# A hybrid decoder step on one core: the first head's q and k of the second attention half loaded in the decode stage

## The chip, the cores and the metric

One Trainium2 chip, one of its cores. The time is device microseconds of one launch of the whole step. Three timed runs of the kernel before gave 1573.43, 1573.64 and 1575.61 us; their median is 1573.64 us.

## The reference

One layer of a decoder. Each token vector (1024 prompt tokens and 8 x 4 sample tokens, 1024 wide) is normalised, modulated and multiplied by one combined input weight, which gives q, k and v of eight attention heads and the inputs of a gated linear recurrence (HGRN). The attention of one head:

```
z = (q @ k.T) * scale + bias_head          # q and k were normalised per head
log_1m = where(key < query, log_sigmoid(-z), 0)
tail   = sum of log_1m over the later keys of the row
w      = where(key < query, exp(log_sigmoid(z) + tail), 0)
o      = w @ v
```

The sample tokens attend to 1024 cached keys each, which lie in pages of 128 keys in DRAM (the decode). Then an output projection with residual, a second norm, and a squared-ReLU MLP (1024 to 4096 to 1024) with residual.

## The kernel before

Every matrix product runs in float32 split into a high and a low part, as three matmuls. The prompt is worked on in two halves of 512 tokens. After q, k and v of all tokens are computed they are put into DRAM scratch: `qkd[part, hi/lo, pair, 128, T]` for q and k, `vd` for v. The order of the stages after that: HGRN with the attention of tokens 0 to 511; output projection of those tokens; then, interleaved, the **first MLP** (tokens 0 to 511, `mlp`, L1178) with `decode_and_attention` (L1434), which is the decode, the HGRN of the sample tokens and the attention of tokens 512 to 1023; then the second output projection and the last MLP.

The interleaving is written by hand: `interleave((mlp(...), WM), (decode_and_attention(), W[3]))` near the end of `hymba_step` draws from two generators in the proportion 64 to 166. From the program so written a planner fixes the order of each engine's instructions and each queue's DMAs beforehand, by simulated times; at run time every engine works through its own list in order. Tiles come from pools; a tile with a `tag` and `bufs=2` has two buffers that later tiles of the tag take in turn when all readers are done. Pools that follow one another lie in the same memory, so a load into a new pool's tile waits for the readers of whatever old tile lay there.

What the change touches:

- `attention` (L874): for each of 8 heads it loads `qh` and `ql` (high and low part of q, 256 KB each, the 64 rows of the head written to both halves of the partitions), `kk` (both parts of k, 512 KB) and `vhl` (v, 512 KB), all issued on GpSimd's queue (L886, L887, L889). Each of the four tiles has two buffers in the pool `attn1`. Then for each block of 128 queries the products `pz` (L900, L901), two sigmoids on ScalarE (L904, L905), masks on GpSimd (L908, L909), a running product on VectorE (L914) and its use on GpSimd (L915), the transposes `ptw` (L927) and the products with v (L936, L937).
- `attn1` lies over the decode's pool: the second buffer of `ql` lies over `ms`, the decode's result, which leaves by the DMA of L696.
- `decode` (L561): GpSimd clears `qbd` (L564), VectorE fills it (L568); pages of 256 KB come on SyncE's queue into four buffers `raw` (L614), are transposed on TensorE (L630) and multiplied with `qbd` (L636).
- `hgrn_decode` (L957): for each of four pairs of heads a transpose `pks` (L991), its copy `kts` by ScalarE (L993) and the products `pds` (L1001) that need it.
- The pool `res` (L1460) beside the first MLP: `xres`, two buffers of 2 KB per partition for the residual in the MLP's last block (L1234, L1235), and `g2b`, 4 KB per partition, the gate (L1183, loaded at L1213). Before they are loaded for that use they lie empty. One buffer of `xres` and part of `g2b` lie over the output projection's last tiles (`hf`, read by L334).
- `weight` (L154): weights come on SyncE's queue (L161) and are split by ScalarE (`whi`, L151) and VectorE or GpSimd (`wlo`, L152).

Of the kernel before, what the change touches and what calls it, by code (L numbers as in the profile page):

```python
# [9 lines left out]
F32 = mybir.dt.float32  # L10
F32R = mybir.dt.float32r
# [9 lines left out]
P = 128  # L21
D = 1024
KT = 8
T = 1024
# [9 lines left out]
NBE0, NBE, NHB, NWA, NU, NRW, NX2, NF = 4,8,3,4,4,4,3,3  # L34
# [47 lines left out]
def hymba_step(ctx, tc, x_p, x_s, ck, cv, st_in, ptab, c_p, c_s, w_ada, b_ada, n1g, n2g, w_in,  # L82
# [3 lines left out]
    V, S, G, TE = nc.vector, nc.scalar, nc.gpsimd, nc.tensor  # L86
# [14 lines left out]
    def pool(name, side="left", stack=ctx, **kw):  # L101
        return stack.enter_context(tc.tile_pool(name=name, bufs=1, side=side, reuse_waits="tile", **kw))
# [7 lines left out]
    qkd = dp.tile([2, 2, 4, P, T], F32, name="qkd")  # L110
# [39 lines left out]
    def split(hi, lo, src, e=None, h=None):  # L150
        (V.tensor_copy if h is V else S.copy)(hi, src)  # L151
        (e or V).tensor_tensor(lo, src, hi.bitcast(F32), op=sub)  # L152
# [34 lines left out]
    def side_by_side(*steps):  # L187

        steps = [[g, n, 0] for g, n in steps]
        while steps:  # L190
            x = min(steps, key=lambda x: (x[2] + 0.5) / x[1])
            if next(x[0], x) is x:
                steps.remove(x)
            else:
                yield
            x[2] += 1
# [38 lines left out]
    def bank(kind, shape, name):  # L235
        turn[kind] = turn.get(kind, -1) + 1
        tag = banks[kind][turn[kind] % len(banks[kind])]
        return psum.tile(shape, F32, name=name, tag=f"bank{tag}", bufs=1)
# [632 lines left out]
        with tc.high_priority(offset=PH):  # L871
            norm()

    def attention(pb, ms, nbe):  # L874

        q0, nq, nk = 256 * ms[0], 256 * len(ms), 256 * (ms[-1] + 1)
        both = lambda t, part, p, r, cs: qkd[t, part, p, r, cs].unsqueeze(0).to_broadcast([2, 64, cs.stop - cs.start])
        for p in range(4):
            for hh in range(2):
                h = 2 * p + hh  # L880
                hr = slice(64 * hh, 64 * hh + 64)

                qh, ql = (pb.tile([P, nq], F32R, name=name, bufs=2) for name in ("qh", "ql"))
                kk_ = pb.tile([P, nk], F32R, name="kk", bufs=2)
                for part, tile_ in enumerate((qh, ql)):
                    G.dma_start(tile_, both(0, part, p, hr, slice(q0, q0 + nq)))  # L886
                G.dma_start(kk_, qkd[1, :, p, hr, 0:nk])  # L887
                vhl = pb.tile([P, nk // P, P], F32R, name="vhl", bufs=2)
                G.dma_start(vhl, vd[0:nk, P * h:P * (h + 1)].rearrange("(t p) x -> p t x", p=P))  # L889
                for m in ms:  # L890
                    ws = []
                    for i in (2 * m, 2 * m + 1):
                        n = (i + 1) * P
                        row, right = [], None
                        for c in reversed(range(0, n, 512)):
                            e = min(n, c + 512)
                            w = e - c
                            pz = bank("z", [P, 512], "pz")[:, :w]
                            qs_ = slice(i * P - q0, (i + 1) * P - q0)
                            TE.matmul(pz, qh[:, qs_], kk_[:, c:e], start=True, stop=False)  # L900
                            TE.matmul(pz, ql[:, qs_], kk_[:, c:e], start=False, stop=True)  # L901
                            om = pb.tile([P, 513], F32, name="om", bufs=NOM)
                            be = pb.tile([P, 512], F32, name="be", bufs=nbe)
                            S.activation(om[:, 0:w], pz, AF.Sigmoid, bias=sbn[:, h:h + 1], scale=-1.0)  # L904
                            S.activation(be[:, 0:w], pz, AF.Sigmoid, bias=sbp[:, h:h + 1])  # L905
                            if right is None:
                                causal = dict(pattern=[[-1, P]], compare_op=ALU.is_gt, base=0, channel_multiplier=1)
                                G.affine_select(om[:, w - P:w], om[:, w - P:w], fill=1.0, **causal)  # L908
                                G.affine_select(be[:, w - P:w], be[:, w - P:w], fill=0.0, **causal)  # L909
                                G.memset(om[:, w:w + 1], 1.0)  # L910
                            else:
                                G.tensor_copy(om[:, w:w + 1], right[:, 0:1])
                            back = om[:, 0:w][:, ::-1]
                            V.tensor_tensor_scan(back, back, back, 1.0 if right is None else right[:, 0:1], op0=mult, op1=ALU.bypass)  # L914
                            G.tensor_tensor(be[:, 0:w], be[:, 0:w], om[:, 1:w + 1], op=mult)  # L915
                            row.insert(0, be)
                            right = om
                        ws.append(row)
                    pv = bank("a", [P, 256], "pv")
                    for kb in range(0, 2 * m + 2, 2):  # L920
                        diag = kb == 2 * m
                        pt = bank("t", [P, 2, 256], "ptw")
                        for a in range(2):
                            for u in range(2):
                                if diag and a == 1 and u == 0:
                                    continue
                                TE.transpose(pt[:, a, u * P:(u + 1) * P], ws[u][kb // 4][:, (kb % 4 + a) * P:(kb % 4 + a + 1) * P], ident)  # L927
                        wh = pb.tile([P, 2, 256], F32R, name="wh", bufs=NWH)
                        wl = pb.tile([P, 2, 256], F32R, name="wl", bufs=NWH)
                        parts = [(slice(0, 1), slice(0, 256)), (slice(1, 2), slice(P, 256))] if diag else [(slice(0, 2), slice(0, 256))]  # L930
                        for a, cs in parts:
                            split(wh[:, a, cs], wl[:, a, cs], pt[:, a, cs], h=V if (kb // 2) % SPL == SPL - 1 else S)
                        for a in range(2):
                            cs = slice(P, 256) if diag and a == 1 else slice(0, 256)
                            vs = vhl[:, kb + a, :]
                            TE.matmul(pv[:, cs], vs, wh[:, a, cs], start=(kb == 0 and a == 0), stop=False)  # L936
                            TE.matmul(pv[:, cs], vs, wl[:, a, cs], start=False, stop=(diag and a == 1))  # L937
                    tv = pb.tile([64, 256], F32, name="tv", bufs=1)
                    S.copy(tv, pv[64:128])
                    V.tensor_tensor(tv, pv[0:64], tv, op=add)  # L940
                    nc.sync.dma_start(mixa[m][64 * h:64 * h + 64, :], tv)
                    yield
# [14 lines left out]
    def hgrn_decode(p1):  # L957
# [63 lines left out]
        for j in range(4):  # L1021
# [10 lines left out]
             lambda n, p=ga: p.tile([P, 2048], F32, name="wada", bufs=NAR)[:, 0:512 * n], "ada")  # L1032
# [4 lines left out]
    qstack.close()  # L1037
    gh = hgrn(pool("hgrn", stack=gstack))
    gb = attention(pool("attn0", stack=astack), (0, 1), NBE0)

    def until(g, x):
# [136 lines left out]
    def mlp(h_hi, h_lo, chunks, fp, nx, side=iter(())):  # L1178
# [1 line left out]
        r_hi = [h_hi[:, k] for k in range(KT)]  # L1180
        r_lo = [h_lo[:, k] for k in range(KT)]
        n = chunks[-1].stop
        g2b = fp.tile([P, D], F32, name="g2b")  # L1183
        acc = [lp.tile([P, HW], F32, name=f"acc{c}", tag="acc", bufs=8) for c in range(KT)]
        for blk in range(NBLK):
            u_hi, u_lo, ws = [], [], []
# [20 lines left out]
            if blk == 0:  # L1207
                for cs in parts:
                    for m in range(NK):
                        up(m, cs)  # L1210
                    yield
            if blk == NBLK - 1:
                nc.sync.dma_start(g2b, g2d.to_broadcast([P, D]))  # L1213
            for half_ in range(2):

# [217 lines left out]

    def decode_and_attention():  # L1434
        banks.update(BD)
        with ExitStack() as es:
            gd = decode(pool("decode", stack=es))
            for _ in range(33):
                next(gd)
                yield  # L1440
            banks.update(BV)
            yield from side_by_side((gd, 28), (hgrn_decode(pool("hgrn_s", stack=es)), W[4]))
        banks.update(BA)
        with ExitStack() as es:
            yield from attention(pool("attn1", stack=es), (2, 3), NBE)

    def h2_tiles():
        return hp2.tile([P, KT, HW], F32R, name="h2_hi", tag="h2_hi", bufs=1), hp2.tile([P, KT, HW], F32R, name="h2_lo", tag="h2_lo", bufs=1)
# [11 lines left out]
    rp = pool("res", side="right", stack=rstack)  # L1460
    banks.update(BM)
    banks.update(m0=M0)
    gate = lambda: rp.tile([P, 512], F32, name="ar", tag="xres", bufs=2)
    ga = ada(AP1, gate, lambda n: wp.tile([P, 512 * n], F32, name="wada", tag="wraw", bufs=NWR), "m")
    interleave((mlp(*h2, [slice(0, 512)], rp, 2, ga), WM), (decode_and_attention(), W[3]))
    h2 = h2_tiles()
    banks.update(o="45", r="36", s=BS)
# [38 lines left out]
```

## Time and profile before

| | |
|---|---|
| median of three runs | 1573.64 us (1573.43 to 1575.61) |
| the profiled execution's own time | 1574.93 us |
| its span (first to last instruction) | 1573.2 us |
| TensorE busy | 1509.9 us, 96% of the span |
| VectorE, ScalarE, GpSimd busy | 1069.0, 641.9, 439.1 us |
| mean granted TensorE clock | 0.985 |
| mean DMA rate over the span | 142 GB/s |

Stages by the span's time: the first MLP with decode and attention runs from about 555 us to 1106 us; the decode's first pages are transposed at 573 us, the first product of the second attention half starts at 832 us. A row of the timeline gives the start, the length, the engine, the line, the operation, the tiles as out<-in, the shapes and, in brackets, how long the engine was idle before and what ended that. DMA issues on a queue carry SPq or POOLq. Where several equal instructions follow one another they share a row with their count.

### The profile page before, as it was taken

How to read it: one execution, taken by the hardware profiler on the slowest of the kernel's cores; microseconds unless marked ns; L12 is line 12 of the kernel's file. 1: busy time of each engine (PE TensorE's matmuls, PEld its weight loads, DVE VectorE, ACT ScalarE, POOL GpSimd, SP SyncE). 2: the span in 40 equal slices, each digit the busy share in tenths (PEclk: the TensorE clock that was granted, in tenths of full speed). 3: DMA queues.
4: the chain of work that ended last, by engine and by line, in shares of the span. 5: the costliest groups of instructions: out<-in, count | busy, mean ns of one | idle time of the engine just before them, and what ended most of it. 6: DMA issues, size and time to landing. Idle time of an engine off the chain costs nothing.

```text
span 1573.2 us, 26210 instructions
## 1 busy us (share of the span) xinstructions
PE 1509.9 (96%) x9485; PEld 1260.8 (80%) x9485; DVE 1069.0 (68%) x2216; ACT 641.9 (41%) x1219; POOL 439.1 (28%) x624
## 2 busy tenths in 40 slices
PE   6999999999999989999998999999798999999998
PEld 3666689998998877765566788888477999999998
DVE  4976438888866872444554987888487657777775
ACT  2742233444423453433232665655344533333340
POOL 0200125644210120000111776793105313331310
PEclk8999999999999999999998999999899999999999
DMA  8379873523124456667566384642743322323222
GB/s 315 121 270 308 264 221 66 111 63 78 39 73 143 135 192 217 206 221 243 157 148 124 97 144 101 133 125 83 228 136 101 104 93 82 103 73 105 84 82 85
DMA packets 249414, 223.14 MB, mean 142 GB/s; under 512 B 60507, under 2 KB 196259, under 8 KB 247236
## 3 DMA queue, kind: packets, MB, share of 16 engines
q1 hardware_dynamic: 186308, 199.26, 40.2%
q0 software_dynamic: 62976, 22.20, 8.2%
q8 instruction: 75, 1.23, 0.3%
q14 instruction: 55, 0.45, 0.1%
HBM read 190.14 MB, written 31.11 MB: 141 GB/s over the span
## 4 chain that ended last, share of the span: by engine, by line
PE 67%; DVE 12%; issue 10%; DMA 6%; ACT 2%; POOL 2%; SPq 0%; POOLq 0%; ACTq 0%; DVEq 0%
PE pm L204 10%; PE pm L205 10%; PE pm L206 10%; PE pm_qkv L217 3%; PE pm_qkv L215 3%; PE pm_qkv L216 3%; PE pm L1223 2%; DVE wlo L152 2%; PE pm L1224 2%; PE pm L1225 2%; PE pm_u L1307 2%; PE pm_u L1308 2%; PE pm_u L1309 2%; PE ptd L630 2%; PE ptw L927 1%
## 5 line engine op out<-in xcount | busy, mean ns | idle before, releaser
L204 PE MATMUL pm<-h_hi,whi 128*128 128x384 f32 (+3 forms) x800 | 273.6, 344 | 7.4 <-DVE h_hi L333 3.3
L205 PE MATMUL pm<-h_lo,whi 128*128 128x384 f32 (+3 forms) x800 | 271.4, 340 | 0.1
L206 PE MATMUL pm<-h_hi,wlo 128*128 128x384 f32 (+3 forms) x800 | 271.2, 340 | 0.0
L151 ACT CAST whi<-wraw 128x1024 fp32r<-128x1024 f32 x136 | 142.7, 1052 | 231.5 <-PE pm L205 114.9
L152 DVE TENSOR_TENSOR wlo<-wraw,whi 128x1024 fp32r<-128x1024 f32 x128 | 171.5, 1340 | 85.4 <-ACT whi L151 76.2
L204 PEld LDWEIGHTS pm<-h_hi,whi 128*128 128x128 f32 x800 | 151.9, 191 | 29.5 <-issue 9.8
L206 PEld LDWEIGHTS pm<-h_hi,wlo 128*128 128x128 f32 x800 | 151.9, 190 | 10.4 <-issue 1.2
L205 PEld LDWEIGHTS pm<-h_lo,whi 128*128 128x128 f32 x800 | 152.0, 190 | 9.1 <-DVE h_lo L334 0.4
L205 PE MATMUL pm<-ul,whi 128*128 128x272 f32 x512 | 146.4, 289 | 2.5 <-DVE ul L1323 2.4
L204 PE MATMUL pm<-uh,whi 128*128 128x272 f32 x512 | 142.0, 290 | 5.3 <-ACT uh L1322 4.3
L206 PE MATMUL pm<-uh,wlo 128*128 128x272 f32 x512 | 145.5, 288 | 0.0
L914 DVE TENSOR_TENSOR_SCAN om<-om 128x128 f32<-128x128 f32 (+3 forms) x96 | 110.0, 1150 | 27.2 <-POOL om L908 19.0
L915 POOL TENSOR_TENSOR be<-be,om 128x384 f32<-128x384 f32 (+3 forms) x96 | 101.2, 1063 | 52.4 <-DVE om L914 43.3
L1223 PE MATMUL pm<-whi,uh 128*128 128x512 f32 x256 | 106.0, 414 | 2.4 <-DVE acc L1231 2.1
L1225 PE MATMUL pm<-whi,ul 128*128 128x512 f32 x256 | 103.0, 406 | 1.6 <-DVE ul L1196 1.6
L1224 PE MATMUL pm<-wlo,uh 128*128 128x512 f32 x256 | 102.4, 401 | 0.0
L205 PEld LDWEIGHTS pm<-ul,whi 128*128 128x128 f32 x512 | 96.3, 188 | 4.0 <-DVE ul L1323 3.9
L204 PEld LDWEIGHTS pm<-uh,whi 128*128 128x128 f32 x512 | 94.0, 188 | 6.7 <-ACT uh L1322 5.0
L206 PEld LDWEIGHTS pm<-uh,wlo 128*128 128x128 f32 x512 | 96.2, 188 | 0.1
L217 PE MATMUL pm_qkv<-whi,h_lo 128*128 128x512 f32 x192 | 77.6, 405 | 0.8 <-DVE h_lo L334 0.8
L215 PE MATMUL pm_qkv<-whi,h_hi 128*128 128x512 f32 x192 | 76.5, 401 | 1.4 <-DVE rs_i L138 1.3
L216 PE MATMUL pm_qkv<-wlo,h_hi 128*128 128x512 f32 x192 | 76.7, 399 | 0.0
(403 smaller groups left out, 3510.2 us busy)
## 6 DMA issues: line engine op xcount, KB each, us to landing
wraw<-in_w_down_dram SPq DMA_DIRECT2D x64, 512.0 KB, 4.0
wraw<-in_w_up_dram SPq DMA_DIRECT2D x40, 512.0 KB, 4.4
wada<-in_w_ada_dram SPq DMA_DIRECT2D x16, 1024.0 KB, 8.1
raw<-in_cache_k_dram SPq DMA_DIRECT2D x64, 256.0 KB, 3.3
vt<-in_cache_v_dram SPq DMA_DIRECT2D x64, 256.0 KB, 3.9
wraw<-in_w_in_dram SPq DMA_DIRECT2D x24, 512.0 KB, 5.0
uraw<-in_w_up_dram SPq DMA_DIRECT2D x24, 512.0 KB, 3.9
wa<-in_w_ada_dram SPq DMA_DIRECT2D x16, 512.0 KB, 6.5
```

What stands on the lines that cost most here:

```text
L151: (V.tensor_copy if h is V else S.copy)(hi, src)
L152: (e or V).tensor_tensor(lo, src, hi.bitcast(F32), op=sub)
L204: TE.matmul(pm, w_hi[:, k, :], r_hi[k][:, cs], start=(k == ks[0]), stop=False)
L205: TE.matmul(pm, w_hi[:, k, :], r_lo[k][:, cs], start=False, stop=False)
L206: TE.matmul(pm, w_lo[:, k, :], r_hi[k][:, cs], start=False, stop=(k == ks[-1]))
L215: TE.matmul(pm, h_hi[:, k, cs], hi, start=(k == 0), stop=False)
L216: TE.matmul(pm, h_hi[:, k, cs], lo, start=False, stop=False)
L217: TE.matmul(pm, h_lo[:, k, cs], hi, start=False, stop=(k == KT - 1))
L914: V.tensor_tensor_scan(back, back, back, 1.0 if right is None else right[:, 0:1], op0=mult, op1=ALU.bypass)
L1223: TE.matmul(pm, u_hi[m][:, ts], hi, start=(m == 0), stop=False)
L1224: TE.matmul(pm, u_hi[m][:, ts], lo, start=False, stop=False)
L1225: TE.matmul(pm, u_lo[m][:, ts], hi, start=False, stop=(m == NK - 1))
```

## The change

The three loads of the first head of the second attention half are issued at the head of `decode_and_attention`, before the decode is set up, into the two `xres` buffers (q) and the `g2b` buffer (k) of the pool `res`. `attention` takes these tiles for its head 0 and loads the other seven heads as before. The loads themselves move into a helper, `load_qk`, with the same access patterns and the same queue. `g2b` is now a tile that is made in the MLP's last block, in the place that `kk0` had. v of head 0 is loaded where it was.

```diff
@@ -871,20 +871,27 @@
-    def attention(pb, ms, nbe):
+    def load_qk(qh, ql, kk, h, q0, nq, nk):
+
+        hr = slice(64 * (h % 2), 64 * (h % 2) + 64)
+        for part, x in enumerate((qh, ql)):
+            G.dma_start(x, qkd[0, part, h // 2, hr, q0:q0 + nq].unsqueeze(0).to_broadcast([2, 64, nq]))
+        G.dma_start(kk, qkd[1, :, h // 2, hr, 0:nk])
+
+    def attention(pb, ms, nbe, first=None):
 
         q0, nq, nk = 256 * ms[0], 256 * len(ms), 256 * (ms[-1] + 1)
-        both = lambda t, part, p, r, cs: qkd[t, part, p, r, cs].unsqueeze(0).to_broadcast([2, 64, cs.stop - cs.start])
...
-                qh, ql = (pb.tile([P, nq], F32R, name=name, bufs=2) for name in ("qh", "ql"))
-                kk_ = pb.tile([P, nk], F32R, name="kk", bufs=2)
-                for part, tile_ in enumerate((qh, ql)):
-                    G.dma_start(tile_, both(0, part, p, hr, slice(q0, q0 + nq)))
-                G.dma_start(kk_, qkd[1, :, p, hr, 0:nk])
+                if h == 0 and first:
+                    qh, ql, kk_ = first
+                else:
+                    qh, ql = (pb.tile([P, nq], F32R, name=name, bufs=2) for name in ("qh", "ql"))
+                    kk_ = pb.tile([P, nk], F32R, name="kk", bufs=2)
+                    load_qk(qh, ql, kk_, h, q0, nq, nk)
...
-        g2b = fp.tile([P, D], F32, name="g2b")
...
             if blk == NBLK - 1:
+                g2b = fp.tile([P, D], F32, name="g2b", tag="g2b")
                 nc.sync.dma_start(g2b, g2d.to_broadcast([P, D]))
...
     def decode_and_attention():
         banks.update(BD)
+        first = [rp.tile([P, n], F32R, name=name, tag=tag, bufs=b)
+                 for name, n, tag, b in (("qh0", 512, "xres", 2), ("ql0", 512, "xres", 2), ("kk0", T, "g2b", 1))]
+        load_qk(*first, 0, 512, 512, T)
...
-            yield from attention(pool("attn1", stack=es), (2, 3), NBE)
+            yield from attention(pool("attn1", stack=es), (2, 3), NBE, first)
```

## Rows read from the trace of the kernel before

**Rows 1.** Waits of PE over the span: total us, times, longest.

```profile
PE pm_os L1103 <- DMA woraw<-in_w_out_dram: 8.2, 1, 8.2
PE pz L900 <- DMA kk<-qkd: 4.9, 1, 4.9
```

**Rows 2.** Timeline of PE around the start of the second attention half.

```profile
832.22 0.45 PE L900 MATMUL pz<-kk,qh 128*128 128x128 f32 x1 [4.88 <-DMA kk<-qkd]
...
833.34 1.12 PE L1001 MATMUL pds<-ve,kts 32*64 32x256 f32 x4
```

**Rows 3.** Windows there: length; busy (count) of PE, PEld, DVE, ACT, POOL; clock; DMA; GB/s.

```profile
827.34:832.22 4.88, 0.01 (x1) 0.04 (x1) 0.00 (x0) 0.92 (x1) 0.00 (x0) 0.71 0.21 57
832.22:839.65 7.43, 7.43 (x21) 5.31 (x21) 3.84 (x6) 0.91 (x4) 3.57 (x7) 0.50 0.79 166
839.65:846.23 6.58, 6.58 (x31) 4.82 (x30) 2.82 (x5) 0.98 (x1) 0.00 (x0) 1.00 1.16 140
```

**Rows 4.** Timeline of POOL: the loads of heads 0 and 1.

```profile
813.69 0.83 POOL L887 DMA_DIRECT2D kk<-qkd  x1
...
833.62 0.78 POOL L886 DMA_DIRECT2D ql<-qkd  x1 [17.32 <-DVE wlo L152]
```

**Rows 5.** DMA issues from 813.6 to 814.2: size, us from issue to landing.

```profile
kk<-qkd POOLq DMA_DIRECT2D x1, 512.0 KB, 18.4
```

**Rows 6.** Timeline of ACT: the cast and the copy ahead of L1001.

```profile
831.30 1.04 ACT L151 CAST whi<-wraw 128x1024 fp32r<-128x1024 f32 x1 [7.20 <-DMA wraw<-in_w_up_dram]
832.26 0.25 ACT L993 COPY kts<-pks 32x128 f32<-32x128 f32 x1
```

**Rows 7.** Timeline of SP: a weight of the MLP issued at 813.78.

```profile
813.78 1.02 SPq L161 DMA_DIRECT2D wraw<-in_w_up_dram  x1
```

**Rows 8.** Windows of the decode's start (columns as in Rows 3).

```profile
570.00:575.00 5.00, 5.00 (x45) 5.00 (x45) 4.78 (x21) 4.24 (x12) 3.96 (x9) 1.00 0.28 61
575.00:580.00 5.00, 5.00 (x43) 4.58 (x46) 4.83 (x11) 1.95 (x5) 0.00 (x0) 1.00 0.93 301
```

**Rows 9.** Waits of DVE from 560 to 600.

```profile
DVE qbd L568 <- POOL qbd L564: 2.1, 1, 2.1
```

**Rows 10.** Timelines of POOL and PE: the decode's setup and its first use.

```profile
566.55 1.65 POOL L334 TENSOR_TENSOR h_lo<-hf,h_hi 128x512 fp32r<-128x512 f32 x1 [8.92 <-DVE h_hi L333]
568.14 1.00 POOL L564 MEMSET qbd<- 128x1088 f32 x1
...
579.74 1.07 PE L636 MATMUL pzd<-kt,qbd 128*32 128x512 f32 x8
```

**Rows 11.** Timeline of SP: loads into the pool `res`.

```profile
568.23 0.33 SPq L1235 DMA_DIRECT2D xres<-x1d  x1
...
582.44 0.43 SPq L1213 DMA_DIRECT2D g2b<-g2d  x1
```

**Rows 12.** DMA issues near 581.1 and near 587.6: one page each.

```profile
raw<-in_cache_k_dram SPq DMA_DIRECT2D x1, 256.0 KB, 3.0
...
raw<-in_cache_k_dram SPq DMA_DIRECT2D x1, 256.0 KB, 6.4
```

**Rows 13.** Timeline of PE: pages 7 and 8, 9 and 13 transposed.

```profile
583.13 1.04 PE L630 MATMUL ptd<-ident,raw 128*128 128x128 f32 x8
...
586.79 0.60 PE L630 MATMUL ptd<-ident,raw 128*128 128x128 f32 x4
...
595.30 0.60 PE L630 MATMUL ptd<-ident,raw 128*128 128x128 f32 x4
```

**Rows 14.** DMA queues from 828 to 831: packets, MB, share of 16 engines.

```profile
q0 software_dynamic: 50, 0.14, 12.8%
q1 hardware_dynamic: 32, 0.01, 2.6%
```

**Rows 15.** The page's median for w_down, and the issue from 834.0 to 834.3.

```profile
wraw<-in_w_down_dram SPq DMA_DIRECT2D x64, 512.0 KB, 4.0
...
wraw<-in_w_down_dram SPq DMA_DIRECT2D x1, 512.0 KB, 8.9
```

## The prediction, before the changed kernel was run

> **What bounds the kernel now.** I read the page first: TensorE is busy for 96% of the span, so a change pays where TensorE stands still or runs slowly, and hardly anywhere else. The list of TensorE's waits comes next [rows 1]. Two waits are long: 8.2 us for the second output projection's weight, which the change does not name, and 4.9 us for `kk`, the k of head 0 of the second attention half. In PE's timeline that wait stands ahead of the first `pz` at 832.22 [rows 2]. The windows add what follows it [rows 3]: in the 4.88 us of the wait TensorE does next to nothing, then it is busy for all of 7.43 us at a granted clock of 0.50, which is the 1.2 GHz level, and from 839.65 on the clock is 1.00, the 2.4 GHz level. 7.43 us at half clock is 3.7 us of work at the full one. So the place costs 4.9 + 3.7 = **8.6 us**, and the change can win no more than that here.
>
> GpSimd issues this k load at 813.69 [rows 4], when the decode's memory comes free, and it lands 18.4 us later [rows 5], at 832.1. A weight of the same 512 KB has a median of 4.0 us [rows 15]. The load is slow and late at once.
>
> **What the change removes at 832.** *The wait for k:* q and k of head 0 are issued about 245 us earlier, so `pz` can start where PE comes to it, at 827.34: **-4.9**.
>
> *The half clock:* the granted clock fell behind a stretch of 4.88 us in which PE did nothing [rows 3]. Without that stretch I expect no fall: **-3.7**. Its bounds are 0 and -3.7.
>
> *What is late next:* `pds`, 1.12 us behind `pz` on PE [rows 2], needs `kts`, a copy on ScalarE. On ScalarE that copy stands behind a cast of the MLP's weight, which began at 831.30 after a wait of 7.20 us for the weight w_up [rows 6]. The weight was issued at 813.78 [rows 7] and so took 17.5 us: it went beside the q and k loads. If PE comes to `pds` at 827.34 + 1.12 = 828.46, the weight must be there by about 827.1 (less 1.04 for the cast, 0.25 for the copy). If it lands at 831.2 as before, `pds` waits until 832.5, 4.1 us, PE stands still nearly as long as before, the clock falls again, and 8.6 shrinks to 4.9 - 4.1 = 0.8. What the weight will take is not in the trace. GpSimd will issue v of head 0 and then q and k of head 1, so loads of the same kind still go beside it, each a little later. The bounds are the 17.5 us of the trace and the 8.9 us that a 512 KB weight took right behind the q and k loads of head 1 [rows 15]. I take 14.3, nearer to the upper end because the neighbours are of the same kind: it lands at 828.1 and `pds` waits **+1.0** (bounds 0 and, with the clock, 7.8).
>
> *Head 1:* its `ql` was issued only at 833.62, after GpSimd had stood for 17.32 us behind a buffer [rows 4]. The buffers turn by one place, so that wait goes to a later head, behind loads that nothing needs soon; I cost it at nothing. The cover is the output of the sample tokens' HGRN, which separates head 0's first product from the rest of the attention. Without it a late `kk` would cost a wait of up to 4.9 again.
>
> **What it adds at 568.** Three issues on GpSimd, 0.83 us each [rows 4], 2.5 us, stand ahead of the clearing of `qbd`. They cannot go before GpSimd's last `h_lo` ends, at 568.2, because one of the q buffers lies over its operand: the load of `xres` into that place was issued at 568.23, just then [rows 10, 11]. VectorE already waits 2.1 us for the cleared `qbd` [rows 9], and is busy for 4.78 of 5 and 4.83 of 5 us in the two windows [rows 8]. TensorE uses `qbd` first at 579.74 [rows 10]. The 2.5 us are mostly covered by that distance; if VectorE's list has no slack they arrive whole. I take **+0.5** (bounds 0 and 2.5).
>
> *The transfers:* 1 MB of q and k is added, where the DMA share is 0.28 until 575 and then 0.93 [rows 8]. The loads of `xres` and `g2b`, issued at 568.23 and 582.44 [rows 11], go away from there and come after head 0 has been used; the MLP's last block, which needs them, stands far behind that, and it is this distance that covers them: I cost them at nothing. Should it be short, the last block would wait one load, 4.0 us [rows 15]. Their going relieves the queue of SyncE by three issues. The pages have little room: one issued at 581.1 took 3.0 us and one at 587.6 took 6.4 [rows 12]; they were used at 586.79 and 595.30 [rows 13], which leaves 2.7 and 1.3 us. A weight beside such loads took 8.9 us for a median of 4.0 [rows 15], so they can make a transfer **4.9 us** late. Less the slack of 2.7 that is **+2.2**. The lower bound is 0: PE waits for none of these pages now, so there is nothing to win. The upper bound is the second rival's 8.9.
>
> **The sum:** -4.9 - 3.7 + 1.0 + 0.5 + 2.2 = -4.9 us. The profiled execution took 1574.93 us and would take 1570.0. The median of the runs, 1573.64, lies 1.3 below it, so I predict 1573.64 - 4.9 = **1568.7 us**. About 0.2% (3.1 us) is what a measurement of this kernel can tell from no change. By itself this case ranges from 1564.5 (all of the gain and a little from the new plan) to 1572.6 (GpSimd's 2.5 and 4.0 of late pages beside the 1.0).
>
> **Rival 1: another wait takes the place.** `pds` waits for `kts`, and this for the weight, as late as before. For it: ScalarE had already stood 7.20 us for that weight [rows 6], which landed 0.9 us before k did. Against it: the weight would no longer go beside the k of head 0. The gain is 0.8; with +0.5 and +2.2 in front the time is 1573.64 - 0.8 + 2.7 = **1575.5**.
>
> **Rival 2: slower, by the pages.** The k load takes its 18 us whatever else happens, and a page that shares its DMA engines ends only when it ends. GpSimd is free at 568.2, issues two q loads, and k at 569.9; with 18.4 us [rows 5] it lands at 588.3. Pages 7 and 8 are transposed at 583.13 [rows 13]; if they come with it, PE waits 5.2 us. The clock would fall as behind the wait of 4.88 (3.7 more), and VectorE's 2.5 would not be covered. That is 11.4, or 8.9 without the 2.5, against a gain of 8.6 - 1.0 = 7.6: +3.8, **1577.4**. It decides from a page lateness of about 4 us in excess of its slack. For it: the weight that took 17.5 us beside k [rows 6, 7] was the same size as two pages. Against it: while the k load was in the way the two queues moved 50 and 32 packets in 3 us [rows 14], so SyncE's queue kept its turn, and the DMA share at 570 to 575 is only 0.28 [rows 8].
>
> The Trainium skill speaks for this rival: the page "DMA: Bandwidth & Descriptors", in "Rules for kernel authors", says that an outermost dimension of a size c below 16 "confines the whole DMA to at most c engines". Both the q loads (two copies) and the k load (two parts) lead with a dimension of 2, so by that rule two engines would carry them, every page with a piece on either would wait there, and the time would be the 1577.4 just worked out. The trace agrees as far as it goes, 18.4 us against 4.0 for the same size [rows 5, 15]; which engines carried the load is in no row here.
>
> **Rival 3: the change does not do what it says.** The order of each engine and queue is planned afresh from simulated times behind 568. The planner may put the three loads late in the decode, or shift other work so that the gain goes into the 8.2 us wait for the output projection's weight [rows 1]. That gives 1573.6, within 3 us on either side. Against it: TensorE is nearly without a wait between the two, so what is won at 832 should arrive.
>
> **How the numbers follow.** The forecast has 0.46, rival 1 0.18, rival 2 0.22, rival 3 0.14. Faster by over 0.2%, under 1570.5: 0.37 of the forecast's 0.46 lies there, 0.02 of rival 1, 0.01 of rival 2, 0.04 of rival 3, together 0.44. Within 0.2%: 0.09 + 0.10 + 0.05 + 0.05 = 0.29. Slower: 0 + 0.06 + 0.16 + 0.05 = 0.27. The range is 1564.0 to 1578.5: it holds the forecast's own range and both rivals' times with about 1 us beyond rival 2, and leaves out pages that are later still (rival 2 with its waits twice) and large gains from the new plan.
>
> **What the profile after would show.** Right: no wait of PE for `kk` near 827, `pz` at a granted clock of 1.00, head 0's q and k issued on GpSimd at 568 to 571, landing long before use. The 1.0 is right if `pds` waits about 1 us and ScalarE's wait for w_up falls to some 4 us. The 2.2 is right if a `raw` page appears among PE's waits between 575 and 600 with about 2 us. Wrong by rival 1: a wait at `pds` of about 4 us released by `kts`, and a clock of 0.50 behind it. Wrong by rival 2: waits for `raw` of 5 us, and 0.50 in a window near 585. Wrong by rival 3: the loads issued far from 568, or a `woraw` wait longer than 8.2 by what was won.

## The result and the profile after

The changed kernel takes 1588.67 us (median of four runs) where the kernel before takes 1574.31: a ratio of 1.0086, with a 95% interval of 1.0070 to 1.0102. That is 14.4 us **slower**, where 4.9 us faster was forecast; it also lies beyond the upper end of the range, 1578.5. The profiled execution has a span of 1588.0 us, 14.8 more than before. One execution of front_spread_wh, below, took 5096.77 us and is left out of its numbers.

PE's waits over the span are the first thing to read (total us, times, longest). PE is TensorE, DVE VectorE, ACT ScalarE, POOL GpSimd and SP SyncE:

```profile
PE pm_os L1110 <- DMA woraw<-in_w_out_dram: 8.2, 1, 8.2
PE ptd L630 <- DMA raw<-in_cache_k_dram: 6.6, 3, 3.1
PE pm L1230 <- DVE acc L1238: 5.6, 3, 4.7
```

The 4.9 us for `kk` [rows 1] are gone, and with them the half clock of [rows 3]. In their place stand 6.6 us for pages of the decode, for which PE did not wait before, and 4.7 us at one time for `acc` (2.1 in all before). The wait for `woraw` is what it was.

**The front.** The DMA issues from 568 to 575 give each load's size and the us from issue to landing:

```profile
kk<-qkd POOLq DMA_DIRECT2D x1, 512.0 KB, 21.4
qh<-qkd POOLq DMA_DIRECT2D x1, 256.0 KB, 7.5
ql<-qkd POOLq DMA_DIRECT2D x1, 256.0 KB, 10.0
...
s0b<-in_state_hgrn_dram POOLq DMA_DIRECT2D x1, 64.0 KB, 18.1
```

GpSimd's issues and PE's transposes of pages, from the timelines:

```profile
569.16 0.90 POOL L878 DMA_DIRECT2D qh<-qkd  x1
...
570.86 0.79 POOL L879 DMA_DIRECT2D kk<-qkd  x1
```

```profile
583.30 0.63 PE L630 MATMUL ptd<-ident,raw 128*128 128x128 f32 x4 [3.08 <-DMA raw<-in_cache_k_dram]
...
586.79 1.09 PE L630 MATMUL ptd<-ident,raw 128*128 128x128 f32 x4 [2.50 <-DMA raw<-in_cache_k_dram]
```

The load of k is issued at 570.86, as forecast, and lands at 592.3. A load of 64 KB of the recurrence's state, issued meanwhile, takes 18.1 us. The windows (length; busy and count of PE, PEld, DVE, ACT, POOL; granted clock; DMA share; GB/s) show what PE pays; the four lines are of the changed kernel, and the line below them is the kernel before, where PE is busy without a gap from 575 to 605 at a clock of 1.00:

```profile
580.00:585.00 5.00, 1.21 (x9) 0.82 (x8) 2.83 (x12) 1.37 (x3) 0.00 (x0) 0.97 1.10 233
585.00:590.00 5.00, 3.21 (x17) 2.94 (x21) 0.69 (x1) 0.00 (x0) 0.00 (x0) 0.50 0.71 154
590.00:595.00 5.00, 5.00 (x28) 2.89 (x21) 1.05 (x1) 2.11 (x4) 0.00 (x0) 0.84 0.42 133
600.00:605.00 5.00, 3.98 (x28) 2.56 (x20) 0.84 (x2) 1.09 (x2) 0.00 (x0) 1.00 0.96 306
```

```profile
585.00:590.00 5.00, 5.00 (x29) 3.16 (x27) 1.79 (x3) 1.80 (x4) 0.00 (x0) 1.00 0.98 316
```

PE stands for 3.79 + 1.79 + 1.02 = 6.6 us. The granted clock is 0.50 for 3.21 us of work (1.6 lost) and 0.84 for 5.00 (0.8 lost). Together that is **9.0 us**. A point that both programs pass is `pzn`, products that stand in both halves of the decode. This view gives count, duration in ns, and the start of the first and the last; first the kernel before, then the changed one:

```profile
L651 PE MATMUL pzn<-kTn,qbf x16: 196/206/217, 667.2 to 744.9; 128*32 128x32 f32 x16
```

```profile
L651 PE MATMUL pzn<-kTn,qbf x16: 196/206/217, 677.0 to 759.9; 128*32 128x32 f32 x16
```

The first comes 9.8 us later, which answers to the 9.0 and to 1.0 that was there before the loads: GpSimd's last `h_lo` begins at 567.57, for 566.55 [rows 10]. The last comes 15.0 later: another **5.2 us** are lost between, where PE has no wait. Of these, 3.3 show in the products of the decode with v: PE is busy with them for 28.3 us before and 31.6 after (L680, from 600 to 830):

```profile
L680 PE MATMUL pod<-vt,wt 128*32 128x512 f32 x128 | 28.3, 602 | 0.0
```

```profile
L680 PE MATMUL pod<-vt,wt 128*32 128x512 f32 x128 | 31.6, 603 | 0.0
```

One such product takes as long as before (602 and 603 ns). 128 of them make 77 us, so they overlap in both kernels, and after the change they overlap less. They also stand in another order, which the planner set anew: on PE, runs of only two such products come 13 times, for 5 times in the kernel before. That pages come late is not the reason, as front_k_spread shows below. The other 1.9 us I cannot assign.

**The start of the second attention half.** GpSimd's timeline:

```profile
829.61 0.84 POOL L879 DMA_DIRECT2D kk<-qkd  x1
847.56 0.93 POOL L896 DMA_DIRECT2D vhl<-vd  x1 [17.11 <-DMA mixs<-ms]
...
850.05 0.34 POOL L915 TENSOR_SCALAR_AFFINE_SELECT om<-om 128x128 f32<-128x128 f32 x1
```

And VectorE's and PE's, a little later:

```profile
850.42 0.42 DVE L921 TENSOR_TENSOR_SCAN om<-om 128x128 f32<-128x128 f32 x1 [6.64 <-POOL om L915]
850.77 0.66 DVE L1238 TENSOR_TENSOR acc<-acc,pm 128x512 f32<-128x512 f32 x1
```

```profile
851.48 0.80 PE L1230 MATMUL pm<-whi,uh 128*128 128x512 f32 x1 [4.70 <-DVE acc L1238]
```

This is a chain over four engines, and is read backwards. PE waits for a bank of PSUM that VectorE's `acc` clears; `acc` stands on VectorE behind head 0's running product; that waits for head 0's mask on GpSimd; and the mask stands behind head 1's v load, which waits 17.1 us until the decode's result `ms`, over whose memory its buffer lies, has left. PE loses 4.7 us, then 1.35 more at half clock:

```profile
851.50:854.20 2.70, 2.70 (x6) 2.13 (x7) 2.05 (x4) 0.00 (x0) 0.54 (x2) 0.50 1.44 332
```

So the account of the profile is 9.0 + 5.2 in front, 8.6 won at 832 and 6.1 lost just behind it: 11.7 of the 14.8 us. Of the other 3, 1.0 was there before the loads, and 1.9 is one wait of PE at 872 for `rr`, which the kernel before does not have.

### The profile page after: what moved, and what is told of

It is laid out like the page before. It is cut to its first block, busy times and chain, and to the rows that moved or that the text cites. A ratio compares the mean times of both kernels' runs of the same rounds, so it can differ in the third digit from the quotient of the medians.

```text
span 1588.0 us, 26219 instructions
## 1 busy us (share of the span) xinstructions
PE 1516.1 (95%) x9485; PEld 1261.6 (79%) x9485; DVE 1077.5 (68%) x2216; ACT 642.9 (40%) x1219; POOL 437.1 (28%) x624
## 4 chain that ended last, share of the span: by engine, by line
PE 71%; DVE 13%; DMA 7%; issue 4%; ACT 2%; POOL 1%; SPq 0%; POOLq 0%; DVEq 0%; ACTq 0%
PE pm L204 10%; PE pm L205 10%; PE pm L206 10%; PE pm_qkv L217 3%; PE pm_qkv L215 3%; PE pm_qkv L216 3%; PE pm L1230 2%; PE pm L1232 2%; PE pm L1231 2%; PE pod L680 2%; DVE wlo L152 2%; PE pm_u L1314 2%; PE pm_u L1315 2%; PE pm_u L1316 2%; DVE om L921 2%
## 5 line engine op out<-in xcount | busy, mean ns | idle before, releaser
L206 PEld LDWEIGHTS pm<-h_hi,wlo 128*128 128x128 f32 x800 | 151.9, 190 | 12.6 <-issue 3.7
```

Source lines behind the costliest of these rows:

```text
L206: TE.matmul(pm, w_lo[:, k, :], r_hi[k][:, cs], start=False, stop=(k == ks[-1]))
```

## The experiments

Two theories were stated. **A:** the load of q and k, in the form in which it is written (a source that leads with a dimension of 2), moves on few DMA engines; whatever needs these engines meanwhile is late. **B:** head 0's masks stand on GpSimd behind a load whose buffer lies over `ms`. The rivals stand with each run. All times are set against runs of the kernel before on the same chip.

**Another form of the early loads (front_spread).** Each early load is cut in two, so that each half goes to 64 partitions and its source leads with a dimension of 64.

```diff
-    def load_qk(qh, ql, kk, h, q0, nq, nk):
+    def load_qk(qh, ql, kk, h, q0, nq, nk, spread=False):
...
+        for half in range(2):
+            for part, x in enumerate((qh, ql)):
+                G.dma_start(x[64 * half:64 * half + 64], qkd[0, part, h // 2, hr, q0:q0 + nq])
+            G.dma_start(kk[64 * half:64 * half + 64], qkd[1, half, h // 2, hr, 0:nk])
...
-        load_qk(*first, 0, 512, 512, T)
+        load_qk(*first, 0, 512, 512, T, spread=True)
```

> The changed kernel, with the three early loads of head 0 cut into six: each writes 64 partitions from a source whose leading dimension is 64. Theory A (the early k load moves on few DMA engines and holds up the cache pages): k lands within about 8 us of its issue instead of 21.4, the pages land in about 5 us, PE's 6.6 us of waits for raw and the half clock near 585 to 595 are gone, and the time falls by some 10 us to about 1578. Rival (the megabyte or the issues on GpSimd are at fault, in whatever form): the pages stay late, GpSimd has three issues more, and the time stays at 1586 to 1591.

Measured: 1572.82 us, ratio 0.9985 (0.9974 to 0.9997). The issues near 567 to 571:

```profile
kk<-qkd POOLq DMA_DIRECT2D x2, 256.0 KB, 4.1
qh<-qkd POOLq DMA_DIRECT2D x2, 128.0 KB, 3.3
ql<-qkd POOLq DMA_DIRECT2D x2, 128.0 KB, 3.4
```

The same bytes, from the same place, at the same time, by the same queue land in 3 to 4 us a piece in place of 7.5 to 21.4, with three issues more on GpSimd. PE has no wait for `raw`, and is busy throughout 575 to 605 at a clock of 1.00. The last `pzn` starts at 744.5, so the 5.2 us behind the front are gone too (L680 takes 28.3 us again), and that is why the gain was 16 us and not the 10 expected. Theory A holds. What keeps this kernel from the forecast is again `acc`: one wait of 4.1 us, behind a wait of GpSimd for `mixs` of 16.3 us.

How few the engines are, the kernel before shows already. From 828 to 831 hardly anything but k's load was left on GpSimd's queue, and the queue's packets took 12.8% of 16 engines' time [rows 14], which is the time of 2.05 engines. From 570 to 573 in front_spread they took 124.1%, the time of 20. The k load is 128 packets of 4 KB in the trace: at most three of them are under way at a time in the kernel before, mostly two, and up to 25 in front_spread. Which engines these are is in no view.

No run separates the leading dimension from the cutting itself. But a load that is not cut speaks for the dimension: in the first attention half of the kernel before, k (leading with 2) and v (leading with 128) have the same size, and each is one load on GpSimd's queue.

```profile
kk<-qkd POOLq DMA_DIRECT2D x8, 256.0 KB, 11.4
vhl<-vd POOLq DMA_DIRECT2D x8, 256.0 KB, 4.3
```

**The early loads alone (before_dead).** The kernel before, with the three early loads added, used by nobody; `g2b` moves into the MLP's last block as in the changed kernel, which the cut below leaves out.

```diff
         banks.update(BD)
+        early = [rp.tile([P, n], F32R, name=name, tag=tag, bufs=b)
+                 for name, n, tag, b in (("qh0", 512, "xres", 2), ("ql0", 512, "xres", 2), ("kk0", T, "g2b", 1))]
+        for part, x in enumerate(early[:2]):
+            G.dma_start(x, qkd[0, part, 0, 0:64, 512:1024].unsqueeze(0).to_broadcast([2, 64, 512]))
+        G.dma_start(early[2], qkd[1, :, 0, 0:64, 0:T])
```

> The kernel before, with the three early loads added at the head of the decode into the same tiles of the pool beside the MLP, but used by nobody; attention loads head 0 as it did. This prices the front alone. Theory A: waits for raw of some 6 us and half clock near 585, the wait for kk of about 5 us at 832 still there: 1573.6 + 10 = about 1584. Rival (the front costs little, and the loss of the changed kernel comes from the end of the decode and from the new plan): 1573 to 1577.

Measured: 1592.36 us, ratio 1.0104 (1.0085 to 1.0124). PE's waits over the span:

```profile
PE ptd L630 <- DMA raw<-in_cache_k_dram: 8.6, 2, 8.2
...
PE pz L900 <- DMA kk<-qkd: 3.1, 1, 3.1
```

The front alone costs 16 us by the ratio, 18 by the medians, in this plan, more than expected: one wait of 8.2 us, half clock behind it, and an order of the decode in which L680 takes 33.0 us. The rival, that the front costs little, is out.

**q or k (front_k_spread).** Of the early loads only k's is cut in two.

> The changed kernel, with only the early k load cut into two of 64 partitions each; the two early q loads keep their form. It tells whether k or q held up the pages. Theory A by size (k is 512 KB on few engines, each q load half of that and on few engines as well): the q loads still take 7 to 11 us and make the first pages late, the waits for raw fall from 6.6 to 0 to 3 us: 1574 to 1580. If k alone was at fault: 1572 to 1574, as with all six. If q alone: 1584 to 1589.

Measured: 1582.54 us, ratio 1.0044 (1.0025 to 1.0063); PE still waits 5.0 us for `raw` (in the trace of 1578.47 us, the fastest of the seven runs). The issues from 565 to 573:

```profile
kk<-qkd POOLq DMA_DIRECT2D x2, 256.0 KB, 13.9
...
qh<-qkd POOLq DMA_DIRECT2D x1, 256.0 KB, 10.2
ql<-qkd POOLq DMA_DIRECT2D x1, 256.0 KB, 12.6
```

It is not k alone. The two q loads, 256 KB each, are enough to make pages late, and they hold up k's halves (13.9 us) although these have the better form. The time lies 2.5 us above the range for fault on both sides and 1.5 below the one for q alone, and far from what k alone would give.

This run also tells what the 5.2 us behind the front are not.

```profile
L651 PE MATMUL pzn<-kTn,qbf x16: 196/206/217, 673.4 to 751.1; 128*32 128x32 f32 x16
```

Pages are late here too, and yet the first and the last `pzn` are 77.7 us apart, as in the kernel before (82.9 in the changed kernel), and L680 takes 28.3 us. Its products stand in runs as in the kernel before. In the other traces the two go together as well: 28.3 us wherever runs of two come 5 times; 31.6 in the changed kernel, layout, after_wh, late_wh and late2_wh, where they come 13 times. So the 5.2 us go with the planner's order and not with late pages. No run held the order fixed.

**Another place in the decode (late_wh, late2_wh).** The early loads in their old form, later. Both kernels also have the layout of after_wh, below.

> The changed kernel with wh over ms, and the three early loads in their old form, written behind the 33rd step of the decode in place of ahead of it. It tells whether the form alone is at fault or the place as well: the pages of the decode's start come just in time, the later ones may have room. If the later pages have room: no wait for raw, no new lateness, and the gain at 832 kept, 1566 to 1570. If a load on few engines delays pages wherever it stands in the decode: a loss of 5 to 10 us near it, 1574 to 1580.

Measured: 1583.74 us, ratio 1.0060 (1.0047 to 1.0073). It missed its purpose: the planner drew the loads forward.

```profile
568.82 0.90 POOL L878 DMA_DIRECT2D qh<-qkd  x1
```

It tells one thing even so. The loads stand behind the clearing of `qbd` here (L564, at 567.44), and PE still waits 8.0 us for `raw`: the issues ahead of that clearing are not at fault. The time lies above both ranges.

The second kernel ties them behind an instruction of GpSimd that comes when the k pages are nearly used up:

```diff
-            G.memset(om[:, NKEY:NKEY + 1], 1.0)
+            mark = G.memset(om[:, NKEY:NKEY + 1], 1.0).ins
+            if gz == 1:
+                with tc.issue_after(mark):
+                    late()
...
+            gd = decode(pool("decode", stack=es), lambda: load_qk(*first, 0, 512, 512, T))
```

> The changed kernel with wh over ms, and the three early loads in their old form queued on GpSimd behind the clearing of one column of dom for the decode's second half, at about 690, when the decode's k pages are used up. If the place matters (the pages there have room): no wait for raw near 585, no half clock there, the lag against the kernel before stays under 2 us until 832, and the time is 1566 to 1571. If a load on few engines costs wherever pages stream: the lag jumps by 5 us or more between 690 and 730, 1572 to 1580.

Measured: 1586.57 us, ratio 1.0073 (1.0058 to 1.0088), above both ranges. GpSimd's timeline, the issue of k from the DMA view, PE's waits and a window:

```profile
675.22 0.85 POOL L881 DMA_DIRECT2D qh<-qkd  x1
...
676.85 0.82 POOL L882 DMA_DIRECT2D kk<-qkd  x1
```

```profile
kk<-qkd POOLq DMA_DIRECT2D x1, 512.0 KB, 20.0
```

```profile
PE ptd L630 <- DMA raw<-in_cache_k_dram: 11.6, 1, 11.6
```

```profile
690.00:700.00 10.00, 2.18 (x8) 1.82 (x9) 0.00 (x0) 0.58 (x1) 0.00 (x0) 0.52 0.59 181
```

The loss moves with the loads. There is nothing near 585; there is one wait of 11.6 us that ends at 697.8, 1 us after k has landed, and half clock behind it. The place does not help: the form costs at both places in the decode where it was tried.

**Nothing moved, another form (before_spread0).** The kernel before; only head 0 of the second half is loaded by six loads, issued where its three were.

> The kernel before, with nothing moved: only head 0's q and k of the second attention half are loaded by six loads of 64 partitions each in place of three. Theory A (what made k late at 832 is the form of the load, not its time of issue): k lands within about 8 us of its issue, before PE comes to it, and the 4.9 us and the half clock go: 1565 to 1569, or about 1572 if kts then waits for the MLP's weight. Rival (it is late because it is issued late): PE's wait for kk stays at 4 us or more, 1573 to 1576.

Measured: 1568.80 us, ratio 0.9972 (0.9957 to 0.9987). The issues from 812.5 to 816.5:

```profile
kk<-qkd POOLq DMA_DIRECT2D x2, 256.0 KB, 6.0
...
qh<-qkd POOLq DMA_DIRECT2D x2, 128.0 KB, 3.5
```

PE waits for nothing from 815 to 860 but 0.5 us. It comes to head 0's `pz` at 831.47, 4 us later than before, because the new plan puts other products ahead of it; but k's second half, issued at 815.40, lands after 7.6 us, at 823.0, in time for 827.34 too. The aim of the change is reached without moving a load: the form of k's load was enough to make it late at 832.

**Theory B: two layouts (layout, after_wh).** In the first, the attention's pool is laid out so that the second buffer of `ql`, head 2's, lies over `ms`.

> The changed kernel, with the buffers of qh, ql and kk allotted ahead of vhl in the attention's pool, so that the second buffer of ql (head 2) and not the second buffer of vhl (head 1) lies over ms. Theory B (head 1's v load stands on GpSimd for 17.1 us and head 0's masks stand behind it): the 17.1 us wait is gone from the front of head 0's masks, so are PE's 4.7 us for acc near 847 and the half clock behind them; 5 to 7 us less, about 1582. The waits for raw near 585 stay at 6 to 7 us. Rival (those 4.7 us come from elsewhere, or another wait takes their place): 1587 to 1590.

Measured: 1587.07 us, ratio 1.0075 (1.0054 to 1.0096): no better than the changed kernel. The rival was right here, the wait only changed its load:

```profile
847.41 0.78 POOL L878 DMA_DIRECT2D ql<-qkd  x1 [16.80 <-DMA mixs<-ms]
848.19 0.30 POOL L920 TENSOR_SCALAR_AFFINE_SELECT om<-om 128x128 f32<-128x128 f32 x1
```

The plan issues head 2's first loads ahead of head 0's masks as well. The second layout puts `wh` over `ms`, which GpSimd does not load and which is first written long after.

```diff
+                    qh = pb.tile([P, nq], F32R, name="qh", bufs=2)
+                    if h == 0 and first:
+                        wh0 = [pb.tile([P, 2, 256], F32R, name="wh", bufs=NWH)]
+                    ql = pb.tile([P, nq], F32R, name="ql", bufs=2)
...
+                        wh = wh0.pop() if first and wh0 else pb.tile([P, 2, 256], F32R, name="wh", bufs=NWH)
```

> The changed kernel, with the attention's pool laid out so that wh, first written some 30 us after head 0's masks, lies over ms, and none of the tiles that GpSimd loads does. Theory B (in the changed kernel GpSimd stands some 17 us in front of head 0's masks because a load's buffer lies over ms): GpSimd's wait for mixs is gone, PE's wait of 4 to 5 us for acc and the half clock behind it too: 5 to 7 us below the changed kernel, 1580 to 1583; the waits for raw near 585 stay at 6 to 8 us. Rival (the masks come late for another reason, or the next wait takes the place): 1586 to 1590.

Measured: 1580.45 us, ratio 1.0039 (1.0024 to 1.0054), 0.47% (7.4 us) under the changed kernel's. The mask now comes right behind the issues:

```profile
830.87 0.87 POOL L878 DMA_DIRECT2D ql<-qkd  x1
831.65 0.40 POOL L923 TENSOR_SCALAR_AFFINE_SELECT om<-om 128x128 f32<-128x128 f32 x1
```

PE's waits of 6.9 us for `raw` stay. Theory B holds, with a little more than the 6.1 us read from the profile. Why GpSimd's wait is so long is less clear. `ms` leaves in four DMAs of 16 KB beside head 1's loads, and the one whose landing is known took 11.0 us; in before_spread0, with head 0's loads in the new form beside them, GpSimd waits 7.6 us for them and not 17.1. That points to theory A again, but it was not tried by itself.

**Both mended (front_spread_wh).**

> The same layout (wh over ms) on the kernel whose three early loads are cut into six. Theory B: PE's 4.1 us for acc near 830 and the half clock behind it go; with the front in order this is the gain that the change was made for, 1572.8 - 6 = about 1567. Rival: a wait of 4 us stays near 830 or comes back before 900, 1571 to 1574.

Measured: 1570.09 us (median of eleven), ratio 0.9972 (0.9958 to 0.9986). This is the gain that was forecast for the change: 4.4 us by the ratio, and by the spans 1573.2 to 1568.4. It needed both faults out of the way. A wait of 0.8 us for `kts` shows here, the term that I had put at 1.0.

**How far the form goes (before_spread, before_spread_both, before_spread0_wh).** The kernel before, nothing moved; the six loads for all heads of the second half, then of both halves, then for head 0 alone with `wh` over `ms`.

> The kernel before, nothing moved, with q and k of all eight heads of the second half only (not the first) in six loads each. If head 0's form was all that mattered: as with head 0 alone, 1567 to 1571. If the later heads' loads hold up weights near the path as well: 1562 to 1566. If GpSimd's 24 further issues cost in the attention, where it works on the masks: 1571 to 1576.

Measured: **1563.97 us**, ratio 0.9933 (0.9921 to 0.9946), the fastest kernel of the study, 10.7 us under the kernel before by the medians. PE has no wait between 815 and 860. GpSimd's further issues do not show.

> The kernel before, nothing moved, with q and k of all heads of both halves loaded by six loads of 64 partitions each in place of three. Theory A (loads that lead with a dimension of 2 move on few DMA engines and hold up whatever shares these): every such load lands within 10 us, the neighbours (weights, mixs) too; 1562 to 1568. Rival (GpSimd, busy in the attention, pays for three more issues per head, 48 in all, or the later heads had room anyway): 1568 to 1574.

Measured: 1587.64 us, ratio 1.0082 (1.0062 to 1.0103): the rival, and worse than it said. The loss begins in the first half, where PE is busy for 46.8 us between 500 and 550 at a clock of 0.90 (49.4 us and 1.00 before). This run's window, columns as above:

```profile
500.00:550.00 50.00, 46.77 (x251) 36.93 (x250) 38.79 (x139) 18.61 (x41) 1.50 (x2) 0.90 0.42 133
```

Whether the issues on GpSimd or the new plan do it was not tried. The plan has a part: in the decode, where this kernel has no such load, L680 takes 33.9 us and PE waits 2.2 us for `raw`.

> The kernel before, nothing moved, head 0's loads of the second half in six, and wh over ms. Theory B says that GpSimd's wait of 7.6 us for mixs, still there with head 0's loads in six, goes as well; head 1's loads then start 8 us earlier beside head 0's. If that wait was costing time: 1564 to 1567. If it was hidden: 1567 to 1570, as without it.

Measured: 1570.73 us, ratio 0.9971 (0.9959 to 0.9983): the same as without the layout. The shorter wait of 7.6 us was hidden.

**Early or in place, all heads in the new form (all_spread_early_wh, all_spread_early2_wh).**

> The changed kernel with wh over ms and with the q and k loads of all eight heads of the second half in six, head 0's early. All three faults that the theories name are gone: 1564 to 1568 if the later heads' form matters, 1568 to 1571 (as with head 0's alone) if it does not, more if GpSimd's further issues cost.

Measured: 1574.93 us, ratio 0.9999 (0.9991 to 1.0008), above both ranges. Head 1 had kept the old form in it, and that gives one more sight of theory A: the MLP's weight beside these loads, issued at 815.77, let its cast begin only at 831.08, and PE waited for `kts`, which hangs on it, as the prediction's first rival has it (and 3.4 us for `rr`):

```profile
PE pds L1022 <- ACT kts L1014: 2.1, 1, 2.1
```

> The changed kernel with wh over ms and all eight heads' q and k loads of the second half in six loads, head 1's too, head 0's early. If the early issue is worth something beside the form: below the 1564.0 of the same loads in place, 1560 to 1563. If the form was all: 1563 to 1567. If the megabyte at the decode's start or the new plan costs something: 1567 to 1573. PE's 2.1 us for kts and the weight's 15.2 us, which all_spread_early_wh showed beside head 1's old loads, should be gone in any case.

Measured: 1566.53 us, ratio 0.9946 (0.9933 to 0.9960). With head 1's loads in the new form too, that wait is gone: the weight beside them, issued at 812.97, is there for its cast at 824.53, which no longer waits for it. The intervals of this kernel and of before_spread overlap; nothing shows that issuing head 0's loads early is worth anything beside their form.

## Why the prediction was wrong

**What held.** The wait for k at 832 and the half clock behind it went, 8.6 us, as their terms said. The loads were issued when the prediction said, behind GpSimd's last `h_lo`. VectorE waited longer for `qbd`, 4.6 us for 2.1 [rows 9], and no wait of PE followed; that term of 0.5 was covered. The 1.0 for `kts` came out at 0 in the changed kernel and at 0.8 in front_spread_wh.

**The term that was mis-sized: late pages, +2.2.** It measured 9.0 us. I took the lateness from one weight beside the q and k loads, 8.9 us for 4.0 [rows 15], and set against it the larger of two pages' slacks, 2.7 and not 1.3. The mechanism was rival 2's, at 0.22, and its price for the front, 8.9 without VectorE's part, was right in the sum: waits of 6.6 us in three places and 2.4 of half clock, where it had 5.2 and 3.7. My own row against it [rows 14] I misread. SyncE's queue did keep its turn, but the 12.8% in that row are two engines' whole time, and that spoke for the rival. Nearer rows were there too: the 17.5 us of a weight beside k [rows 6, 7] were what the pages were to meet.

The Trainium skill had the rule: the page "DMA: Bandwidth & Descriptors", "Rules for kernel authors", asks for an outermost dimension that is a multiple of 16. The runs agree: with 64 outermost the two halves of the k load take 3.7 and 4.6 us, in place of 21.4 for the whole. I cited it for the rival and let the sum go by the milder row.

**What had no term: the planner's new order, 5.2 us.** The decode's products with v overlap less in it. Rival 3 named a plan that shifts other work, but only for a time within 3 us of no change, and the sum had nothing for it.

**The step that failed outright: head 1, costed at nothing.** "The buffers turn by one place, so that wait goes to a later head, behind loads that nothing needs soon". The buffers did not turn. Head 0's tiles left the pool, so `vhl` was allotted first, and its second buffer came to lie over `ms`. And the wait stood ahead of head 0's masks, on the engine that makes them. Before, that order cost nothing, because head 0's `pz` waited just as long for k: removing the one wait laid the other bare. I had named what waits on GpSimd and not what stands behind it there: 6.1 us by the profile, 7.4 by the run.

Without these three the number is met, 1570.1 against 1568.7, but in part by luck. In front_spread_wh no page is late for PE, so 2.2 and 0.5 drop out and the terms that are left give -4.9 - 3.7 + 0.8 = -7.8. That much stands in its trace at the second output projection, whose first `pm_os` begins at 1107.1, for 1114.9 (0.8 of it was there before the loads). At the end of the span 4.8 is left: 3 us are lost behind 1107, where the forecast had no term.

## What to carry to other kernels

Before moving a slow load to an earlier place, ask why it is slow: here 512 KB took 18 us because the source leads with a dimension of 2, and with 64 in front each half took 4 to 8. At 568, at 677 and at 814 this load made others late beside it, and moving it only chose who pays. The cure has to be measured place by place as well: in the second half it won 10.7 us, in both halves it lost 12.6.

When a wait goes, read the list of the engine that issues: a load that waits for its buffer also holds back every computation behind it in that engine's order, and a changed set of tiles in a pool can change which load that is. And where a planner fixes the order of the engines, compare the order before and after, before time is put down to what the chip did.

## What was not expected of the hardware

- One load in the old form slows small transfers as much as large ones: 64 KB of state took 18.1 us beside the early loads and 2.3 before; 512 KB of weight took 17.5 beside k [rows 6, 7] with a median of 4.4.
- Loads in the better form suffer from a neighbour in the worse: k's halves took 13.9 us behind the old q loads, and 4.1 without them.
- On GpSimd an issue of a 64-partition load takes 0.5 to 0.6 us, for 0.83 of one whole, so the six took 3.1 us (812.81 to 815.90) and the three take 2.5:

```profile
812.81 0.56 POOL L889 DMA_DIRECT2D qh<-qkd  x1
813.34 0.58 POOL L889 DMA_DIRECT2D ql<-qkd  x1
```
